# A two-layer decoder trunk on one core: an explicit list of steps, a planned issue order on every engine, and layer 0's values as weights in column tiles

## The chip, the cores and the metric

The kernel runs on one core of a Trainium2 chip. The metric is the device time of one execution in microseconds (us); less is better. Before the change the median of three runs is 644.46 us (641.27 to 646.58).

## The reference, cut to what matters

Two layers work on 256 tokens of width 1024. Layer 0 mixes tokens by blockwise attention with 16 heads of 64 columns; one block holds all 256 tokens here, so it is plain causal attention. Layer 1 mixes by differential attention: 8 heads, each with two score maps and a value of 128 columns. A squared-ReLU MLP of inner width 4096 follows each. Every sub-layer's input is scaled and shifted by vectors made from the conditioning vector `c`, and its output is gated by a third.

```python
mod = jnp.einsum('bd,lde->lbe', jax.nn.silu(c), ada_w) + ada_b[:, None, :]
for i in range(DEPTH):
    shift1, scale1, gate1, shift2, scale2, gate2 = [m[:, None, :] for m in jnp.split(mod[i], 6, axis=-1)]
    h = x * (1.0 + scale1) + shift1
    ...
        y = moba_attention(h, moba_w_in[j], moba_w_out[j])
    ...
        y = diff_attention(h, diff_w_in[j], diff_w_out[j], ...)
    x = layer_norm(DEEPNORM_ALPHA * x + (1.0 + gate1) * y, ln_g[i, 0], ln_b[i, 0])
    h = x * (1.0 + scale2) + shift2
    y = sq_relu_mlp(h, mlp_w_up[i], mlp_w_down[i])
    x = layer_norm(DEEPNORM_ALPHA * x + (1.0 + gate2) * y, ln_g[i, 1], ln_b[i, 1])
```

In layer 0 a head is `p = softmax(q k^T / 8 + causal)`, `o = p v`. In layer 1 it is `w = softmax(q1 k1^T) - lam * softmax(q2 k2^T)`, `o = w v`, then an RMS norm of `o`.

## The kernel before, in words

Tokens stand in two blocks `b` of 128 rows. Every dense product is made of three products of rounded operands: each float32 matrix is split into `hi` (rounded by ScalarE, L131) and `lo` (the rest, by VectorE, L132), and TensorE adds `xh*wh + xh*wl + xl*wh` (L168 to L170 for one PSUM bank, L185 for two). Weights arrive by DMA into three `raw` buffers of 1 MB and are split into eight `hi` and eight `lo` buffers. Scores (L451), transposes through the identity (L400, L431, L510, L321, L116, L705) and the product of probabilities and values (L491) are plain float32 matmuls; the profile shows two records for each of the score and value matmuls.

The work is named by steps, which the string `PROGRAM` lists by layer. V, Q: a 512-column product for values, or for queries and keys of four heads (`g` is the group of four). T: transposes of queries and keys. S: scores and softmax of one block `b` and group `g`. P: transposes of the probabilities, products with the values. F: transposes of the result into operands `sTh`, `sTl` of the output projection. O: output projection. B and C: the gate is spread over the partitions (L116), then LayerNorm and the next modulated input. U, X: MLP up and its transposes. Y: an up step for both blocks at once, with the weights stationary (L724, L729). D: MLP down. E: the last downs of block 1, cut in columns.

The vectors made from `c` cost 96 rows of work: for each of 12 vectors and 8 column blocks, a 0.5 MB DMA into `aw` (two buffers, L216) and a multiply-and-sum on VectorE (L217). Sixteen of them belong to the first layer's input; the other 80 stand in a queue of fillers, `f3` in the list takes three from it, and `need` empties it as far as a step demands.

SP issues all loads and stores, in order. An engine's own queue is in order too: an instruction that waits holds all behind it. Within that, the order in which the instructions of each engine stand is made at build time by the framework's scheduler, which takes the program order as priority; the kernel marks the later scores of a block as urgent and keeps them in program order.

Softmax of layer 0 leaves `p` unnormalised; `sums` (L465, its reciprocal) is applied to the product by VectorE at L502, so the transposes of `p` need only the exponentials. For one head, `p` transposed (128 keys by 128 queries) is the stationary operand and 64 columns of `v` move:

```python
pe.matmul(op[:, h], lhsT=pT[i][kb], rhs=vn[kb, g // 2][:, v0 + h.start:v0 + h.stop], ...)
```

Of the kernel before, what the change touches and what calls it, by code (L numbers as in the profile page):

```python
# [73 lines left out]
def tile_trunk(ctx: ExitStack, tc: tile.TileContext, x, c, moba_w_in, moba_w_out, diff_w_in, diff_w_out,
# [145 lines left out]
    def queue_vector(l, v):  # L220
        cl = small.tile([P, KC], F32, name=f"col{l}{v}")

        def step(j):
            return lambda: ada_rows(l, v, j, cl[:, j:j + 1], "aw", 2)

        def fin():
            if v in (SCALE1, GATE1, SCALE2, GATE2):
                vec.tensor_scalar(out=cl, in0=cl, scalar1=1.0, scalar2=None, op0=ALU.add)
            cols[l, v] = cl

        for j in range(KC):
            filler.append(step(j))
        filler.append(fin)
# [594 lines left out]
```

## Time and profile before

| | us |
|---|---|
| median of 3 runs | 644.46 |
| span of the profiled execution | 639.4 |
| TensorE matmuls busy | 609.9 (95%) |
| VectorE busy | 501.2 (78%) |
| ScalarE busy | 377.4 (59%) |

The page and the times give no device time of the profiled execution beyond its span; the median of the runs is 5.1 us above the span and the fastest run 1.9 us. Matmuls are drawn longer than the distance to the next one (a 512-column matmul about 395 ns, with the next one starting 227 ns later), so the busy share hides gaps of up to some 170 ns: starts are what counts. By time, layer 0's attention ends at about 155 us, its MLP at about 320, layer 1's attention at about 445 and its MLP at about 620; the last 19 us hold the end of the last down projection, LayerNorm and the stores.

### The profile page before, as it was taken

Reading aid. Unit: us, or ns where it says so; the run is one execution under the profiler, and the core shown is the slowest. Engines: PE = TensorE matmul, PEld = TensorE weight load, DVE = VectorE, ACT = ScalarE, POOL = GpSimd, SP = SyncE. Lnnn points to the kernel's source line nnn. Section 1 sums busy time; section 2 is a strip of 40 time slices with the busy share of each in tenths; the row PEclk is TensorE's granted clock in tenths of the full one; section 3 lists DMA queues with packets and bytes.
Section 4 is the critical chain, followed back from the end, with each engine's and each line's share of the span. In section 5 each row is a group of like instructions: output and inputs, shape, how many; then the busy total and the mean of one; then the engine's idle time right before and its main releaser. Section 6 shows DMA issues by size and latency. Waiting matters only on the chain.

```text
span 639.4 us, 8821 instructions
## 1 busy us (share of the span) xinstructions
PE 609.9 (95%) x3164; PEld 501.8 (78%) x3164; DVE 501.2 (78%) x907; ACT 377.4 (59%) x699; POOL 21.2 (3%) x36
## 2 busy tenths in 40 slices
PE   4989999998999999999999999999999999999995
PEld 3767887886888888888877787767788888888884
DVE  5798998979978987887799889877984645565447
ACT  3448666657746564655477676775785556465530
POOL 0000000011000000000000010021100000000001
PEclk9999999999999999999999999999999999999998
DMA  8987988976689988888765967782663764646501
GB/s 294 406 312 288 313 321 292 309 251 224 226 285 361 331 316 312 316 300 335 257 227 189 337 230 242 253 283 66 206 218 109 260 225 152 244 147 202 194 0 67
DMA packets 66086, 158.25 MB, mean 248 GB/s; under 512 B 4057, under 2 KB 21370, under 8 KB 66042
## 3 DMA queue, kind: packets, MB, share of 16 engines
q1 hardware_dynamic: 66042, 157.68, 70.2%
q8 instruction: 25, 0.41, 0.2%
q14 instruction: 19, 0.16, 0.1%
HBM read 156.62 MB, written 1.05 MB: 247 GB/s over the span
## 4 chain that ended last, share of the span: by engine, by line
PE 59%; DVE 21%; DMA 10%; ACT 3%; issue 3%; POOL 2%; SPq 1%; DVEq 0%; ACTq 0%; POOLq 0%
PE ac L185 13%; PE sc L185 10%; DMA aw<-in_ada_w_dram 8%; PE mm L724 7%; PE tp L724 6%; DVE lo L132 6%; DVE aw L217 5%; PE mm L170 4%; PE mm L729 3%; PE mm L168 3%; PE mm L169 3%; PE tp L729 3%; DVE z L293 1%; ACT hi L131 1%; DVE z L290 1%
## 5 line engine op out<-in xcount | busy, mean ns | idle before, releaser
L132 DVE TENSOR_TENSOR lo<-raw,hi 128x1024 fp32r<-128x1024 f32 x196 | 232.1, 1197 | 47.5 <-ACT hi L131 43.6
L131 ACT CAST hi<-raw 128x1024 fp32r<-128x1024 f32 x196 | 201.2, 1034 | 67.0 <-PE sc L185 46.4
L217 DVE CUSTOM_DVE_ANT_0 aw<-aw,sbc,tabT 128x1024 f32<-128x1024 f32 x96 | 121.9, 1279 | 16.4 <-DMA aw<-in_ada_w_dram 16.0
L168 PE MATMUL mm<-hi,hT 128*128 128x512 f32 x224 | 90.6, 405 | 5.3 <-ACT hi L131 2.5
L170 PE MATMUL mm<-hi,hT 128*128 128x512 f32 x224 | 89.1, 398 | 0.0
L169 PE MATMUL mm<-lo,hT 128*128 128x512 f32 x224 | 88.8, 397 | 0.2 <-DVE lo L132 0.2
L724 PE MATMUL mm<-hT,hi 128*128 128x512 f32 x192 | 60.4, 396 | 0.0
L724 PE MATMUL tp<-hT,hi 128*128 128x512 f32 x192 | 60.3, 395 | 0.0
L168 PEld LDWEIGHTS mm<-hi,hT 128*128 128x128 f32 x224 | 42.3, 189 | 15.2 <-ACT hT L555 3.0
L185 PE MATMUL ac<-hi,sTh 128*128 128x512 f32 x160 | 51.2, 397 | 0.0
L185 PE MATMUL ac<-lo,sTh 128*128 128x512 f32 x160 | 50.8, 393 | 0.0
L185 PE MATMUL ac<-hi,sTl 128*128 128x512 f32 x160 | 50.4, 392 | 0.0
L170 PEld LDWEIGHTS mm<-hi,hT 128*128 128x128 f32 x224 | 42.4, 189 | 9.1 <-DVE hT L329 0.4
L169 PEld LDWEIGHTS mm<-lo,hT 128*128 128x128 f32 x224 | 42.4, 189 | 8.6 <-DVE lo L132 0.3
L185 PE MATMUL sc<-hi,sTh 128*128 128x512 f32 x144 | 45.3, 392 | 0.0
L185 PE MATMUL sc<-lo,sTh 128*128 128x512 f32 x144 | 45.2, 391 | 0.0
L185 PE MATMUL sc<-hi,sTl 128*128 128x512 f32 x144 | 44.6, 391 | 0.0
L729 PEld LDWEIGHTS tp<-hT,lo 128*128 128x128 f32 x192 | 34.4, 188 | 7.5
L729 PEld LDWEIGHTS mm<-hT,lo 128*128 128x128 f32 x192 | 34.4, 188 | 7.3
L734 ACT COPY nat<-mm 128x256 f32<-128x256 f32 x24 | 7.8, 376 | 52.4 <-PE mm L724 52.4
L729 PE MATMUL tp<-hT,lo 128*128 128x256 f32 x192 | 36.0, 279 | 0.0
L729 PE MATMUL mm<-hT,lo 128*128 128x256 f32 x192 | 35.9, 279 | 0.0
(169 smaller groups left out, 909.4 us busy)
## 6 DMA issues: line engine op xcount, KB each, us to landing
aw<-in_ada_w_dram SPq DMA_DIRECT2D x96, 512.0 KB, 5.5
raw<-in_mlp_w_up_dram SPq DMA_DIRECT2D x32, 1024.0 KB, 5.5
raw<-in_mlp_w_down_dram SPq DMA_DIRECT2D x32, 1024.0 KB, 4.9
raw<-in_diff_w_in_dram SPq DMA_DIRECT2D x16, 512.0 KB, 4.9
raw<-in_moba_w_in_dram SPq DMA_DIRECT2D x24, 256.0 KB, 5.9
raw<-in_moba_w_in_dram SPq DMA_DIRECT2D x8, 512.0 KB, 4.7
raw<-in_moba_w_out_dram SPq DMA_DIRECT2D x4, 1024.0 KB, 7.8
raw<-in_diff_w_in_dram SPq DMA_DIRECT2D x4, 1024.0 KB, 6.2
```

The lines of the kernel that those rows point to most:

```text
L131: act.copy(out=hi[:, :n], in_=raw_ap)
L132: vec.tensor_tensor(out=lo[:, :n], in0=raw_ap, in1=hi[:, :n], op=ALU.subtract)
L168: pe.matmul(dst, lhsT=xh, rhs=wh, start=start, stop=False)
L169: pe.matmul(dst, lhsT=xh, rhs=wl, start=False, stop=False)
L170: pe.matmul(dst, lhsT=xl, rhs=wh, start=False, stop=stop)
L185: pe.matmul(dsts[h], lhsT=a, rhs=w[:, h * 512:(h + 1) * 512], start=start and k == 0 and i == 0, stop=stop and k == n - 1 and i == 2)
L217: vec.tensor_tensor_reduce(out=aw, in0=aw, in1=sbc, scale=1.0, scalar=adab_cols(l, v)[:, j:j + 1], op0=ALU.mult, op1=ALU.add, accum_out=dst)
L290: vec.tensor_tensor(out=z[:, c_], in0=accs[c_.start // 512][:, a0:a0 + c_.stop - c_.start], in1=gate[:, c_], op=ALU.mult)
L293: vec.scalar_tensor_tensor(out=z[:, c_], in0=xt[b][:, c_], scalar=ALPHA, in1=z[:, c_], op0=ALU.mult, op1=ALU.add)
L724: pe.matmul(ps, lhsT=w[k][0][:, c_], rhs=x3[k], start=first, stop=last)
L729: pe.matmul(ps[:, 0:S], lhsT=w[k][1][:, c_], rhs=x3[k][:, 0:S], start=False, stop=False)
L734: act.copy(out=r[:, i * S:(i + 1) * S], in_=ps[:, S:2 * S])
```

## The change

Three things change.

First, the list. One list of explicit steps replaces the two: a step names its layer, the filler queue is gone and each of its 80 rows is a step of its own (`a024`: layer 0, vector 2, column block 4), weight loads are steps of their own (`q02`, `o00`, `u03`, `d05`), and B is cut into G (gate), K (rows of the LayerNorm's weights) and N (scale and shift columns); R is the residual. Steps of the next stage stand inside the one before.

Second, the order. The instructions are recorded in the order of the list, and then `plan_issue` walks them with a table of durations and latencies: of the instructions whose inputs and buffers its own clock says are ready, each engine takes the first in the list. `issue_in_order` then ties each instruction to the one before it on its engine, on all five of them. The urgent marks on the scores go. On TensorE the planner keeps half-array matmuls next to each other.

Third, layer 0's values. `attend_values_T` multiplies `p` by the reciprocal sums on ScalarE ahead of the transposes, and then makes the transposed result directly: 64 columns of `v` are the stationary operand, the 128 queries move, and two heads write the two halves of the partitions (column tiles of 64). So layer 0 has no F step and no multiplication by `sums` on VectorE; `split_oT` reads the product where it read the transposes.

```diff
-    L0 V00 V10 Q00 T00 Q10 T10 Q01 T01 Q11 T11 S0 V01 f2 S1 f1 P0 S2 V11 f5 P1 F0 S3 P2 Q02 T02 f4 S4
...
+    Q001 V000 a031 a037 a030 T001 Q000 Q011 S02 a024 a042 a022 q02 a021 T011 S03 a025 Q010 T010 T000 V010 S01
...
+    def forward(self, prio, wait_ns=0.0):
...
+            c = cand[e]
+            pick = None
+            if e == 4 and pair[lastpe] and lastpe + 1 < N and pair[lastpe + 1]:
+                for x in c:
+                    if x[1] == lastpe + 1 and x[2] <= t + 60:
+                        pick = x
+            if pick is None:
+                lim = t + wait_ns
+                pick = min([x for x in c if x[2] <= lim])
...
+def plan_issue(ins, slots, psum_names):
+    p = Planner(ins, slots, psum_names)
+    p.forward(list(range(p.N)))
+    return p.orders
...
+def pairable(i):
+    return not i.is_transpose and tuple(i.tile_size) in ((64, 128), (128, 64))
+
+
+def issue_in_order(tc, ins, orders):
+    for o in orders:
+        for a, b in zip(o, o[1:]):
+            tc.add_manual_dep(ins[b], ins[a].name,
+                              mybir.DependencyInfo(mybir.DependencyClass.NoSync, mybir.DependencyReason.DATA),
+                              reason="planned order")
...
+    def step_ada(st, l, v, j):
+        if (l, v) not in cols:
+            cols[l, v] = small.tile([P, KC], F32, name=f"col{l}{v}")
+        cl = cols[l, v]
+        ada_rows(l, v, j, cl[:, j:j + 1], "aw", 2)
...
-                    first = i == kb == 0 and cpt == 1
-                    with nullcontext() if first else tc.high_priority():
-                        mm = pe.matmul(r[i, cpt][:, kb * P:(kb + 1) * P], lhsT=qk[b, g][rows, i, :],
-                                       rhs=qk[kb, g][rows, 2 + i, :], start=True, stop=True)
-                        if not first:
-                            tc.keep_in_program_order(mm)
+                    pe.matmul(r[i, cpt][:, kb * P:(kb + 1) * P], lhsT=qk[l, b, g][rows, i, :],
+                              rhs=qk[l, kb, g][rows, 2 + i, :], start=True, stop=True)
...
+    def attend_values_T(b, g, ps_, sums):
+        n = P * (b + 1)
+        v0 = (g % 2) * 256
+        oT_ps = psum("ac" if g < 2 else "mm")
+        for i in range(2):
+            pair = ps_[2 * i:2 * i + 2]
+            for cpt, pt in enumerate(pair):
+                c_ = 2 * i + cpt
+                act.activation(out=pt[:, :n], in_=pt[:, :n], func=AF.Copy, scale=sums[:, c_:c_ + 1])
+            pT = probs_T(b, pair)
+            for kb in range(b + 1):
+                for cpt in range(2):
+                    h0 = v0 + (2 * i + cpt) * HD
+                    pe.matmul(oT_ps[cpt * HD:(cpt + 1) * HD, i * P:(i + 1) * P], lhsT=vn[0, kb, g // 2][:, h0:h0 + HD],
+                              rhs=pT[cpt][kb], start=kb == 0, stop=kb == b)
+        split_oT(0, b, g, oT_ps)
...
+    ins = [i for i in nc.cur_bb.bb.instructions if i.opcode != "TilePoolBoundary"]
+    issue_in_order(tc, ins, plan_issue(ins, slots, psum_names))
```

The order moves at three places that the prediction speaks of. On TensorE, at the end of layer 0's attention, the rows before are these (L431 transposes `p`, L491 multiplies by the values, L510 transposes the result, L185 is the output projection into `ac` for block 0 and `sc` for block 1).

```order
L185 MATMUL ac<-lo,sTh 128x512 x2
L185 MATMUL ac<-hi,sTl 128x512 x2
L431 MATMUL tp<-cs,p 128x128 x8
L185 MATMUL sc<-hi,sTh 128x512
L491 MATMUL mm<-v,pT 128x64 x8
L510 MATMUL tp<-cs,on 128x128 x2
L185 MATMUL sc<-hi,sTh 128x512
L185 MATMUL sc<-lo,sTh 128x512
L510 MATMUL tp<-cs,on 128x128 x2
L185 MATMUL ac<-hi,sTh 128x512 x2
```

The rows at the same place now (L765 transposes `p`, L852 multiplies by the values, L538 is the output projection):

```order
L538 MATMUL sc<-hi,sTh 128x512 x2
L765 MATMUL tp<-cs,p 128x128 x2
L538 MATMUL sc<-lo,sTh 128x512
L765 MATMUL tp<-cs,p 128x128 x2
L538 MATMUL sc<-lo,sTh 128x512
L765 MATMUL tp<-cs,p 128x128 x2
L538 MATMUL sc<-hi,sTl 128x512
L765 MATMUL tp<-cs,p 128x128 x2
L538 MATMUL sc<-hi,sTl 128x512
L852 MATMUL mm<-pT,v 64x128 x4
L538 MATMUL sc<-hi,sTh 128x512 x2
```

The transposes of the result are gone, the transposes of `p` stand between matmuls of the output projection, and block 0's projection (`ac`) is over before the last transposes of `p`, where twelve of its matmuls stood behind them before.

On VectorE, at the end of layer 1's attention, the rows before (L217 are rows of the conditioning vectors, L476 and L473 finish a softmax, L502 normalises a result, L520 splits it):

```order
L502 TENSOR_TENSOR on<-mm,ss 128x256
L476 SCALAR_TENSOR_TENSOR p<-p,sums_4144 128x256
L217 ISA aw,col_526<-aw,sbc,tabT 128x1024
L217 ISA col_526 128x1
L473 RECIPROCAL sums_4157<-sums_4157 128x2
L474 TENSOR_TENSOR sums_4157<-sums_4157,nlam 128x1
L520 SCALAR_TENSOR_TENSOR sTl<-tp,sgcol,sTh 128x2x128
L217 ISA aw,col_526<-aw,sbc,tabT 128x1024
L217 ISA col_526 128x1
L476 SCALAR_TENSOR_TENSOR p<-p,sums_4157 128x256
```

and now (L803, L804 and L806 finish a softmax, L834 normalises, L873 splits):

```order
L834 TENSOR_TENSOR on<-mm,ss 128x256
L804 TENSOR_TENSOR sums_4220<-sums_4220,nlam 128x1
L803 RECIPROCAL sums_4233<-sums_4233 128x2
L804 TENSOR_TENSOR sums_4233<-sums_4233,nlam 128x1
L806 SCALAR_TENSOR_TENSOR p<-p,sums_4220 128x256
L806 SCALAR_TENSOR_TENSOR p<-p,sums_4233 128x256
L873 SCALAR_TENSOR_TENSOR sTl<-tp,sgcol,sTh 128x2x128
```

The rows of the conditioning vectors have left this place. Of the 96 rows in the whole order, 40 stand up to the end of layer 0's first LayerNorm before and now; 36 follow up to layer 0's second LayerNorm before, and 42 now; 20 stand from there to layer 1's first LayerNorm before, and 14 now.

On SP, in layer 0's MLP, the rows before:

```order
L146 DMA raw<-in_mlp_w_up_dram 128x4x512
L216 DMA aw<-in_ada_w_dram 128x1024 x2
L146 DMA raw<-in_mlp_w_up_dram 128x4x512
L216 DMA aw<-in_ada_w_dram 128x1024
L160 DMA raw<-in_mlp_w_down_dram 128x2x1024
```

and now:

```order
L562 DMA aw<-in_ada_w_dram 128x1024 x2
L513 DMA raw<-in_mlp_w_down_dram 128x2x1024
L562 DMA aw<-in_ada_w_dram 128x1024 x4
L513 DMA raw<-in_mlp_w_down_dram 128x2x1024
L562 DMA aw<-in_ada_w_dram 128x1024
```

Up to four loads into `aw`, which has two buffers, now stand ahead of a weight load.

More of the change, by code (lines that the diff above doesn't have):

```diff
@@ L62, in _schedule @@
+"""
 def _schedule():
-    for part in PROGRAM:
-        for t in part.split():
-            yield (t[0],) + tuple(int(d) for d in t[1:])
+    for t in PROGRAM.split():
+        yield (t[0],) + tuple(int(d) for d in t[1:])
 SHIFT1, SCALE1, GATE1, SHIFT2, SCALE2, GATE2 = range(6)
@@ L70, with __init__, tile, _access @@
 C_W = 576
+class SlotPool:
+    def __init__(self, pool, slots):
+        self.pool, self.slots = pool, slots
+    def tile(self, shape, dtype, tag=None, name=None, bufs=1):
+        t = self.pool.tile(shape, dtype, tag=tag or name, name=name, bufs=bufs)
+        self.slots[(t.tensor if hasattr(t, "tensor") else t).name] = (tag or name, bufs)
+        return t
+def _access(a):
+    a = getattr(a, "bass_ap", None)
+    if a is None:
+        return None
+    t = a.tensor
+    if type(t).__name__ != "Tile":
+        return None
+    size = 1
+    for n in t.shape[1:]:
+        size *= n
+    p0, f0 = divmod(a.offset, size)
+    np_ = a.ap[0][1]
+    pm = 0
+    for q in range(p0 // 32, (p0 + np_ + 31) // 32):
+        pm |= 1 << q
+    g = max(1, size // 64)
+    free = [(s, n) for s, n in a.ap[1:] if n > 1 and s]
+    run = free.pop()[1] if free and free[-1][0] == 1 else 1
+    offs = [f0]
+    for s, n in free:
+        offs = [o + s * i for o in offs for i in range(n)]
+    fm = 0
+    for o in offs:
+        lo, hi = o // g, (o + run - 1) // g
+        fm |= ((1 << (hi - lo + 1)) - 1) << lo
+    return t.name, pm, fm
@@ new lines, in _transfer, with run @@
+def _transfer(i):
+    o, s_ = i.outs[0], i.ins[0]
+    def run(dims):
+        r = 1
+        for s, n in reversed(dims):
+            if n > 1:
+                if s != r:
+                    break
+                r *= n
+        return r
+    store = type(s_.bass_ap.tensor).__name__ == "Tile"
+    on, off = (s_, o) if store else (o, s_)
+    r = run(list(on.ap)[1:])
+    if not any(s == 0 and n > 1 for s, n in off.ap):
+        r = min(r, run(list(off.ap)))
+    return o.ap[0][1] * _elems(o) / r / 16 * (8 + r * 4 * 0.0368) * 1.03
@@ L125, in tile_trunk @@
         xt.append(xb)
+    xs = {(b, 0): xt[b] for b in range(2)}
     def split_piece(raw_ap, n=1024):
@@ L218, in ada_rows @@
                                  op0=ALU.mult, op1=ALU.add, accum_out=dst)
[L220 to L233, printed above, removed]
-    def need(key):
-        while key not in cols:
-            fill()
+    def step_ada(st, l, v, j):
[3 more added lines that the diff above has]
+        ada_rows(l, v, j, cl[:, j:j + 1], "aw", 2)
+        if j == KC - 1 and v in (SCALE1, GATE1, SCALE2, GATE2):
+            vec.tensor_scalar(out=cl, in0=cl, scalar1=1.0, scalar2=None, op0=ALU.add)
     def affine_cols(l, first, prev):
         sc, sh = (l, SCALE1 if first else SCALE2), (l, SHIFT1 if first else SHIFT2)
-        need(sc)
-        need(sh)
         A = small.tile([P, KC], F32, name=f"A{l}{int(first)}")
@@ L638, in close @@
             return
[L639 to L641 removed]
+        z = layer_norm(b, accs, gate, xs[b, 2 * l + i])
+        modulate(b, z, *st["ab", l, i], tiles)
+        st["z", l, i, b] = z
     def run(program, st):
```

476 lines of the change are left out of this document (352 added, 124 removed).

## The prediction

> **What bounds the kernel now.** I read the busy times by stretch first, then TensorE's groups, then TensorE's timeline where stages meet, then the rows of VectorE. Columns of the stretches: length, then busy time of PE, PEld, DVE, ACT and POOL with counts, granted clock, DMA share, GB/s.
>
> ```profile
> 0.00:40.00 40.00, 29.18 (x115) 22.23 (x115) 28.51 (x55) 17.20 (x33) 0.29 (x5) 1.00 0.96 357
> 40.00:160.00 120.00, 115.50 (x660) 92.52 (x660) 108.63 (x253) 77.99 (x176) 3.30 (x4) 1.00 0.81 283
> 160.00:320.00 160.00, 160.00 (x808) 135.68 (x807) 133.20 (x181) 91.76 (x130) 0.00 (x0) 1.00 0.85 304
> 320.00:460.00 140.00, 133.65 (x707) 105.59 (x706) 124.58 (x288) 95.96 (x225) 15.02 (x24) 1.00 0.65 225
> 460.00:620.00 160.00, 160.00 (x808) 135.40 (x808) 91.34 (x103) 93.48 (x138) 0.00 (x0) 1.00 0.53 180
> 620.00:639.40 19.40, 11.56 (x76) 10.39 (x73) 14.90 (x30) 1.02 (x2) 2.55 (x3) 0.90 0.15 55
> ```
>
> Both MLPs (160 to 320, 460 to 620) keep TensorE busy without a gap. The first 40 us run at a DMA share of 0.96. What is left to win lies in the two attentions, 40 to 160 and 320 to 460: TensorE shows 4.50 + 6.35 us idle there, and VectorE 11.4 + 15.4 us, so VectorE is nearly as full as TensorE.
>
> Idle by the page is not all, since a matmul's row is drawn beyond the start of the next. So I count slots from start to start. The chain of waits gives the wide one, the timeline at 606 us a period of two wide and two half-wide matmuls, and the one at 70 us the small ones.
>
> ```profile
> 260.99 5.45 PE ac L185 x24
> 266.44 5.44 PE sc L185 x24
> ```
>
> ```profile
> 606.32 0.40 PE L729 MATMUL tp<-hT,lo 128*128 128x256 f32 x2
> 606.55 0.63 PE L724 MATMUL tp<-hT,hi 128*128 128x512 f32 x2
> ...
> 607.02 0.39 PE L729 MATMUL tp<-hT,lo 128*128 128x256 f32 x2
> ```
>
> ```profile
> 69.26 0.40 PE L170 MATMUL mm<-hi,hT 128*128 128x512 f32 x1
> 69.59 0.49 PE L451 MATMUL sc<-qkT 64*128 64x128 f32 x2
> 70.00 0.51 PE L168 MATMUL mm<-hi,hT 128*128 128x512 f32 x1
> ...
> 74.37 0.40 PE L170 MATMUL mm<-hi,hT 128*128 128x512 f32 x1
> 74.70 1.16 PE L451 MATMUL sc<-qkT 64*128 64x128 f32 x16
> 75.79 2.00 PE L491 MATMUL ac<-v,pT 128*128 128x64 f32 x16
> 77.62 0.39 PE L510 MATMUL tp<-cs,on 128*128 128x128 f32 x2
> ```
>
> A wide slot is 5.45/24 = 0.227 us; the period is 0.70. Sixteen value records (L491) take 1.83, 0.114 each. A burst of score matmuls in half arrays costs 0.10 to enter (74.70 - 74.37 - 0.227) and 1.09 for 16 records, 1.19 for 8 matmuls; a burst of one costs 0.10 + 0.41 = 0.51. Between these, a burst of m matmuls is about 0.41 + 0.0975 m.
>
> ```profile
> L168 PE MATMUL mm<-hi,hT 128*128 128x512 f32 x194 | 77.6, 401 | 1.9 <-ACT hT L328 1.1 <-ACT hT L555 0.8
> ...
> L185 PE MATMUL ac<-hi,sTh 128*128 128x512 f32 x96 | 31.4, 401 | 0.0
> ...
> L724 PE MATMUL mm<-hT,hi 128*128 128x512 f32 x96 | 30.2, 396 | 0.0
> ...
> L729 PE MATMUL tp<-hT,lo 128*128 128x256 f32 x96 | 18.0, 279 | 0.0
> ...
> L451 PE MATMUL sc<-qkT 64*128 64x128 f32 x192 | 16.9, 291 | 0.0
> ...
> L321 PE MATMUL tp<-cs,z 128*128 128x128 f32 x44 | 6.9, 280 | 3.2 <-DVE nm L311 1.8 <-DVE z L309 1.5
> L510 PE MATMUL tp<-cs,on 128*128 128x128 f32 x32 | 6.4, 281 | 1.4 <-ACT gate L118 0.7 <-DVE sums L473 0.5 <-DVE on L502 0.2
> ```
>
> These are groups between 40 and 460 us. There are 618 wide matmuls on L168 to L170 (three lines of 194 and twelve of each third in `sc` and `ac`), 576 on L185 (six groups of 96), 192 and 192 in L724 and L729, and 396 narrow ones. Slots: 1194 x 0.227 = 271.0; 96 periods of 0.70 = 67.2; 396 x 0.11 = 43.6; the scores, in 20 bursts of the old order (four of 1, three of 3, five of 4, one of 7, seven of 8), 17.6. Sum 399 of 420 us: about 20 us of waits, of which the MLP between them has hardly 1. The releasers named beside L321 and L510 are VectorE and ScalarE; nothing waits for a weight load by DMA.
>
> **Part 1, layer 0's values on TensorE.** Before: 48 matmuls, two records each, 96 x 0.114 = 10.9 us. Now they come in twelve bursts (two of 2, nine of 4, one of 8). No row shows column tiles; the nearest are the row tiles of the scores. By those: 2 x 0.61 + 9 x 0.80 + 1.19 = 9.6. Sixteen transposes go, 16 x 0.11 = 1.8. The scores come in 23 bursts now (twelve of 2, four of 4, seven of 8): 18.8, so +1.2. Together -1.3 - 1.8 + 1.2 = **-2 us**. The upper end is no overlap between tiles: 10.9 again plus twelve switches of 0.3, +3. The lower end is a free switch: the 16 records of 1.09 us give 0.068 each, 6.5 in all, and then -5.
>
> The Trainium skill ("TensorEngine Tiling (Array Packing)", Theoretical Speedup) allows up to twice the rate where one side is 64; halving 10.9 would make the part -6, and no run here shows it yet.
>
> **Part 2, VectorE in the attentions.**
>
> ```profile
> 40.00:160.00 120.00, 35.78 (x56) 1.00 0.81 283
> 160.00:320.00 160.00, 46.11 (x72) 1.00 0.85 304
> 320.00:460.00 140.00, 25.58 (x40) 1.00 0.65 225
> ```
>
> ```profile
> L502 DVE TENSOR_TENSOR on<-mm,sums 128x256 f32<-128x256 f32 x4 | 1.7, 423 | 2.7 <-PE mm L491 2.7
> L502 DVE TENSOR_TENSOR on<-ac,sums 128x256 f32<-128x256 f32 x4 | 1.7, 418 | 0.0
> ```
>
> The first three rows are L217 alone, two records a row of work: 25.58/20 = 1.28 us. Six such rows leave layer 1's attention, 7.7 us. L502 leaves layer 0's, 3.4 us. With as much idle time on VectorE as now, 26.8 us, the two stretches would shrink by these 11.1. TensorE allows it: it has some 19 us of waits there. The order adds a little at the LayerNorm of layer 0, where L321 and its like wait: between the end of block 0's projection and the transposes of its LayerNorm stood 45 wide slots, 10.2 us; now 42, eight transposes of `p`, two bursts and four transposes of the gate, 9.5 + 0.9 + 1.6 + 0.4 = 12.4. I take 2 of the 3.2 us. Together **-13 us**, -2 of which are the chance of the new order and the rest of the load. Ends: -1 (waits only change places) and -19 (all of them go).
>
> **Part 3, what is added, and what hides it.** ScalarE multiplies 32 maps in layer 0.
>
> ```profile
> L475 ACT ACTIVATE p<-p,sums 128x256 f32<-128x256 f32 x8 | 4.1, 507 | 1.5 <-DVE sums L474 1.4
> ...
> L475 ACT ACTIVATE p<-p,sums 128x128 f32<-128x128 f32 x8 | 3.2, 402 | 1.0 <-DVE sums L474 1.0
> ```
>
> 16 x 0.507 + 16 x 0.402 = 14.5 us on an engine with 78 of 120 busy: hidden if TensorE has other work. It lies in the chain, though: the transposes of a pair needed two exponentials, and now need four, their reciprocal and two products (price below). Six more L217 rows in layer 0's MLP make 7.7 us on VectorE, 133.2 to 141 of 160, and 3.1 MB more for the DMA, share 0.85 to about 0.90, below the 0.96 of the first stretch: hidden, 0; if that cover goes, up to 8. The runs of four `aw` loads ahead of a weight load hold SP until VectorE has freed two buffers, about 4 x 1.28 = 5 us, while the weights ahead of it feed a period of two sets of 48 wide slots, 22 us. The first 40 us load the same bytes in nearly the same order: 0, ends -1 and +1. The tail has the same VectorE steps behind the last matmul: 0.
>
> **Sum.** -2 - 13 = -15 against the span of 639.4: 624. The median of the runs is 5 us above the span; scaled, 644.5 x 624.4/639.4 = 629. The unknown costs span -5 - 19 - 1 = -25 to +3 - 1 + 8 + 1 = +11.
>
> **Rivals.**
>
> Same: VectorE sets both attentions and the new order only moves the waits, as any in-order queue with 1.2 us steps may. For it: VectorE is 90% busy in both. Against: six rows and L502 do leave. It gives part 1 and 2 to 3 us, 640.
>
> Slower: the longer softmax chain is not covered in layer 0.
>
> ```profile
> L418 ACT ACTIVATE p<-sc,mx 128x256 f32<-128x256 f32 x32 | 15.0, 476 | 7.8 <-DVE mx L415 7.0 <-DVE sums L474 0.6
> L415 DVE CUSTOM_DVE_ANT_0 sc<-sc,cs 128x256 f32<-128x256 f32 x32 | 13.2, 436 | 1.0 <-ACT p L418 0.9
> ...
> L418 ACT ACTIVATION_READ_ACCUMULATOR p<-sc,mx 128x1 f32 x64 | 12.9, 202 | 0.0
> ...
> L415 DVE DVE_READ_ACCUMULATOR2_ANT mx<- 128x1 f32 x64 | 9.0, 141 | 0.0
> ...
> L465 DVE RECIPROCAL sums<-sums 128x4 f32<-128x4 f32 x8 | 1.4, 173 | 0.6 <-ACT p L418 0.5
> ```
>
> For block 1 the two extra maps cost 2 x (0.436 + 0.141) on VectorE and one exponential with its sum, 0.68, then 0.17 and 2 x 0.507: 3.0 us more before the transposes; I take 2.7 over both blocks. Eight times is 22, and with layer 1's 8 us still won and part 1 kept the end is 644 + 22 - 10 = 656. It decides where fewer than about 4 x 0.58 + 0.68 + 0.17 + 1.0 = 4.2 us of other matmuls stand between scores and transposes. At the last block 15 wide slots, sixteen transposes and two value bursts stand there, 3.4 + 1.8 + 1.6 = 6.8 us: against it.
>
> Column tiles that don't overlap.
>
> ```profile
> L491 PEld LDWEIGHTS mm<-v,pT 128*128 128x128 f32 x72 | 9.0, 191 | 1.4 <-ACT pT L433 1.1
> ```
>
> If the load of one tile's weights can't run beside the other tile's matmul, a pair of records takes 0.19 + 0.11 = 0.30; 48 pairs and twelve switches of 0.3 make 18.0, 7.1 more than before, and part 1 becomes +6.5: 644.5 - 6.5 = 638. The Trainium skill ("TensorE: Matmul & The Clock Gate", What overlaps and what doesn't) says that weight loads overlap running matmuls only where the row groups differ, and two column tiles share all their rows. The rows here, with tiles that differ in rows, can't tell.
>
> **How the numbers follow.** About 1% is what a measurement of this kernel can tell from no change: 638 to 651. Forecast, 620 to 637: 0.62. Column tiles that don't overlap, 638: 0.08, half of it faster. Same, 640: 0.20. Slower, 656: 0.08. All waits gone and tiles at full rate, below 620: 0.02. So faster 0.68, within 1% 0.24, slower 0.08. The range reaches from just under the forecast's end to the cases of no change: 618 to 643.
>
> **What would show it.** Right: TensorE's busy time falls to about 601 (624 less 19 at both ends and 4 in the attentions), VectorE's by 3.4 in all; the stretch that was 320 to 460 shortens by 8 or more, that of layer 0's attention by 4 or more; layer 0's MLP stays at 160 us with TensorE full; the value matmuls come 0.07 us apart in a burst. Wrong: TensorE waits on ScalarE's scaled `p` or on weights in layer 0's MLP; VectorE idles more than 27 us in the attentions; or value matmuls stand 0.11 us apart or more.

## The result and the profile after

The changed kernel takes 650.19 us (median of 4 runs, 649.63 to 650.67) against 642.87 for the kernel before on the same chip: a ratio of 1.0115 (95% interval 1.0077 to 1.0153). It is slower by about 1%; 629 was forecast, with a range of 618 to 643. The profiled execution has a span of 647.8 us, 8.4 more than before.

The busy times by stretch of the changed kernel, with columns as before:

```profile
40.00:160.00 120.00, 116.14 (x639) 88.40 (x638) 103.19 (x241) 87.13 (x205) 5.02 (x4) 0.99 0.80 280
160.00:320.00 160.00, 152.95 (x758) 125.68 (x757) 136.22 (x186) 90.94 (x130) 0.00 (x0) 1.00 0.87 313
320.00:460.00 140.00, 138.00 (x728) 111.41 (x727) 116.22 (x276) 94.20 (x223) 17.34 (x22) 1.00 0.61 210
460.00:620.00 160.00, 159.84 (x806) 134.19 (x806) 92.53 (x107) 93.18 (x139) 2.49 (x2) 1.00 0.54 185
```

Layer 0's MLP, where TensorE had 808 matmul records in 160 us, now has 758. At the mean distance of 160/808 = 0.198 us the 50 missing ones are 9.9 us. Layer 1's MLP is untouched (806 against 808). To see whole stages, I take the time from the first transposes of block 1's LayerNorm to those of block 0's next one. For layer 0's MLP these are two rows of TensorE's timeline before,

```profile
154.59 0.33 PE L321 MATMUL tp<-cs,z 128*128 128x128 f32 x1 [0.47 <-DVE z L309]
...
325.56 0.41 PE L321 MATMUL tp<-cs,z 128*128 128x128 f32 x2 [0.95 <-DVE nm L311]
```

and two after:

```profile
156.55 0.33 PE L654 MATMUL tp<-cs,z 128*128 128x128 f32 x1
...
338.05 0.41 PE L654 MATMUL tp<-cs,z 128*128 128x128 f32 x2 [1.72 <-DVE nm L644]
```

So the stage was 171.0 us and is 181.5. Read off in the same way:

| stage, us | before | after |
|---|---|---|
| start to the end of layer 0's attention | 154.6 | 156.6 |
| layer 0's MLP | 171.0 | 181.5 |
| LayerNorm | 13.0 | 12.7 |
| layer 1's attention | 107.8 | 104.0 |
| LayerNorm | 13.0 | 12.7 |
| layer 1's MLP | 171.9 | 172.2 |
| from the last matmul to the end | 8.1 | 8.1 |

Three stages are longer by 10.5, 2.0 and 0.3 us, the others shorter by 3.8 and 0.6: 8.4 in all. The loss is nearly all in one stage, layer 0's MLP; the gain of layer 1's attention is half the forecast one, and layer 0's attention gained nothing. The conditioning rows moved as the order said (L563 alone, two records a row; before 56, 72 and 40):

```profile
40.00:160.00 120.00, 35.68 (x56) 0.99 0.80 280
160.00:320.00 160.00, 48.85 (x79) 1.00 0.87 313
320.00:460.00 140.00, 21.70 (x34) 1.00 0.61 210
```

What waits in layer 0's MLP between 160 and 320 us (engine, line, what ended the wait: total us, times, longest) was this before,

```profile
DVE aw L217 <- DMA aw<-in_ada_w_dram: 11.1, 7, 4.3
```

and is this after:

```profile
DVE aw L563 <- DMA aw<-in_ada_w_dram: 16.0, 13, 2.5
...
ACT hi L484 <- DMA raw<-in_mlp_w_down_dram: 6.7, 3, 3.3
PEld ac L538 <- DVE lo L485: 5.9, 5, 2.0
...
PE ac L538 <- DVE lo L485: 3.8, 4, 1.5
```

VectorE stands longer and more often at a row whose data has not landed; the weight splits (`lo`, L485) are queued behind that row on VectorE, and now TensorE waits for them, which it hardly did before. One such place, first on VectorE and then on TensorE (the first number is the start, the one in brackets the wait):

```profile
222.77 1.28 DVE L563 CUSTOM_DVE_ANT_0 aw<-aw,sbc,tabT 128x1024 f32<-128x1024 f32 x1 [1.80 <-DMA aw<-in_ada_w_dram]
...
223.98 1.22 DVE L485 TENSOR_TENSOR lo<-raw,hi 128x1024 fp32r<-128x1024 f32 x1
```

```profile
225.25 0.73 PE L538 MATMUL ac<-lo,sTh 128*128 128x512 f32 x2 [1.55 <-DVE lo L485]
```

The other change is in the scores. The timeline of TensorE in the changed kernel at three bursts, each with what follows it:

```profile
75.96 0.66 PE L852 MATMUL ac<-pT,v 128*64 128x128 f32 x8
76.55 0.50 PE L522 MATMUL mm<-lo,hT 128*128 128x512 f32 x1
...
77.92 1.71 PE L783 MATMUL sc<-qkT 64*128 64x128 f32 x16
79.56 0.50 PE L521 MATMUL mm<-hi,hT 128*128 128x512 f32 x1
...
82.12 0.71 PE L783 MATMUL sc<-qkT 64*128 64x128 f32 x4 [1.59 <-ACT p L752]
82.75 0.50 PE L521 MATMUL mm<-hi,hT 128*128 128x512 f32 x1
```

Eight records of the column tiles (L852) take 76.55 - 75.96 = 0.59 us, and the two records of a pair start 6 to 7 ns apart: the two tiles overlap. But these sixteen records of the scores take 1.64, where the prediction's row gave 1.09, and four take 0.63. The old order let the two halves of the array take turns. In the new one the marks that kept the scores in program order are gone, and the planner takes whichever half has a free bank, so several matmuls of one half follow each other and don't overlap (the first five records of this burst start 111 ns or more apart). Counted from start to start with their entries, the scores take 24.2 us instead of 18.1, the column-tile values 9.1.

### The profile page after: what moved, and what is told of

The parts are those of the page before. It is cut to its first block, busy times and chain, and to the rows that moved or that the text cites. A ratio compares the mean times of both kernels' runs of the same rounds, so it can differ in the third digit from the quotient of the medians.

```text
span 647.8 us, 8858 instructions
## 1 busy us (share of the span) xinstructions
PE 615.0 (95%) x3148; PEld 498.2 (77%) x3148; DVE 498.6 (77%) x899; ACT 387.4 (60%) x731; POOL 27.7 (4%) x36
## 4 chain that ended last, share of the span: by engine, by line
PE 58%; DMA 16%; DVE 15%; issue 4%; ACT 4%; POOL 2%; SPq 0%; DVEq 0%; ACTq 0%; POOLq 0%
PE ac L538 11%; DMA aw<-in_ada_w_dram 11%; PE sc L538 9%; PE mm L522 5%; PE mm L521 5%; PE mm L523 5%; DVE lo L485 5%; DVE aw L563 4%; PE mm L1069 4%; PE tp L1069 4%; DMA raw<-in_moba_w_in_dram 3%; PE sc L783 3%; ACT hi L484 2%; PE tp L1074 2%; PE mm L1074 2%
## 5 line engine op out<-in xcount | busy, mean ns | idle before, releaser
L485 DVE TENSOR_TENSOR lo<-raw,hi 128x1024 fp32r<-128x1024 f32 x196 | 231.0, 1198 | 61.4 <-ACT hi L484 59.9
L563 DVE CUSTOM_DVE_ANT_0 aw<-aw,sbc,tabT 128x1024 f32<-128x1024 f32 x96 | 121.9, 1281 | 27.0 <-DMA aw<-in_ada_w_dram 26.9
L522 PE MATMUL mm<-lo,hT 128*128 128x512 f32 x224 | 90.5, 405 | 0.7 <-DVE lo L485 0.7
L538 PE MATMUL ac<-lo,sTh 128*128 128x512 f32 x160 | 50.9, 398 | 3.8 <-DVE lo L485 3.8
L538 PE MATMUL ac<-hi,sTh 128*128 128x512 f32 x160 | 50.7, 397 | 1.5 <-ACT hi L484 1.5
L538 PE MATMUL ac<-hi,sTl 128*128 128x512 f32 x160 | 51.2, 397 | 0.0
L522 PEld LDWEIGHTS mm<-lo,hT 128*128 128x128 f32 x224 | 42.7, 190 | 10.4 <-DVE lo L485 2.1
L538 PE MATMUL sc<-hi,sTl 128*128 128x512 f32 x144 | 45.8, 394 | 1.4 <-DVE sTl L1086 1.4
L538 PE MATMUL sc<-hi,sTh 128*128 128x512 f32 x144 | 46.2, 395 | 0.0
L538 PE MATMUL sc<-lo,sTh 128*128 128x512 f32 x144 | 45.8, 392 | 0.0
L538 PEld LDWEIGHTS ac<-lo,sTh 128*128 128x128 f32 x160 | 29.3, 188 | 11.7 <-DVE lo L485 5.9
```

What stands on the lines that cost most here:

```text
L485: vec.tensor_tensor(out=lo[:, :n], in0=raw_ap, in1=hi[:, :n], op=ALU.subtract)
L522: pe.matmul(dst, lhsT=xh, rhs=wl, start=False, stop=False)
L538: pe.matmul(dsts[h], lhsT=a, rhs=w[:, h * 512:(h + 1) * 512], start=start and k == 0 and i == 0, stop=stop and k == n - 1 and i == 2)
L563: vec.tensor_tensor_reduce(out=aw, in0=aw, in1=sbc, scale=1.0, scalar=adab_cols(l, v)[:, j:j + 1], op0=ALU.mult, op1=ALU.add, accum_out=dst)
```

## The experiments

Two theories for the MLP came first: **rows** (42 instead of 36 conditioning rows are too many for that stage) and **landing** (the time from a load's issue until its data can be used: the fixed order places rows on VectorE by a landing of 4.0 us, `1530 + 1310 + 1150` ns, which the loads don't keep). The rest of the loss was to be **pairing** of the scores or the **chain** (ScalarE's products ahead of the transposes). All kernels compute the whole reference. Ratios are to the kernel before on the same chip; "MLP 0", "att 1" and so on are the stages of the table, from one profiled execution each.

### One part alone on the old kernel

**e_columns**: only `attend_values_T`.

```diff
+        if kind == 0:
+            return attend_values_T(b, g, ps_, sums)
```

> The kernel before, with layer 0's values in column tiles alone (scaled p, no F step in layer 0), order by the framework's scheduler. If the column tiles overlap as the changed kernel's trace shows (a burst of four matmuls 0.68 to 0.80 us with its entry, 96 records in 8.7 us against 10.7) and sixteen transposes go (1.8), TensorE loses about 4 us: 639 against 643, less if VectorE sets layer 0's attention (641). If the longer softmax chain (exponentials, reciprocal, two products) is what cost the change its time, 646 or more.

Measured: 642.92, ratio 1.0008 (0.9985 to 1.0031). The first two stretches:

```profile
40.00:160.00 120.00, 111.38 (x639) 85.65 (x639) 105.86 (x244) 87.17 (x205) 3.30 (x4) 0.99 0.80 281
160.00:320.00 160.00, 160.00 (x807) 135.63 (x807) 133.28 (x181) 92.49 (x132) 0.00 (x0) 1.00 0.85 303
```

TensorE is busy 4.1 us less in layer 0's attention (115.50 before) and VectorE 2.8 us less, and the stage is no shorter (156.3 at its end, 154.6 before). The work that leaves both engines doesn't come back as time. Of TensorE's waits between 40 and 160 us the two longest are these; the longest before was 1.1 us:

```profile
PE ac L185 <- DVE lo L132: 2.9, 1, 2.9
PE mm L522 <- ACT pT L433: 2.2, 1, 2.2
```

The first is for a weight split, and the granted clock behind it is 0.51 from 107 to 110.5 us (1.00 before), 1.7 us more. The second is the column tiles (L522) waiting for ScalarE's copies of the transposed `p`. So ScalarE has its extra 9 us, and a chain that costs 22 is refuted; 2.2 us of it can be seen, and with the split they use up the gain of this execution.

**e_halves**: the old kernel with its scores half by half.

```diff
-        for i in range(2):
-            for kb in range(b + 1):
-                for cpt in (1, 0):
-                    rows = slice(cpt * 64, (cpt + 1) * 64)
+        for cpt in (1, 0):
+            rows = slice(cpt * 64, (cpt + 1) * 64)
+            for i in range(2):
+                for kb in range(b + 1):
```

> The kernel before, with the score matmuls recorded half by half: all of rows 64 to 127 first, then all of rows 0 to 63, instead of in turn. Theory 'halves': matmuls in the same half do not overlap, a burst of 16 records takes 1.73 us with its entry instead of 1.18 and one of 8 records 1.19 instead of 0.75; 8 x 0.55 + 8 x 0.44 = 8 us more on TensorE, the time 5 to 8 us longer (648 to 651). Rival: TensorE waits in the attentions anyway, the time at most 2 us longer.

Measured: 643.66, ratio 1.0029 (1.0009 to 1.0049); scores 21.8 us instead of 18.1. Unpaired scores cost the old order 2 us, less than expected: the 3.7 us partly fill waits.

### Pairing, rows and landing in the changed kernel

**e_pair**: the planner keeps the scores in list order and starts a group only when both banks are free.

```diff
+        rows = [k for k in range(N) if self.pair[k] and ins[k].tile_size[0] == 64]
+        self.heads = set(rows) - {k + 1 for k in rows}
+        for j, k in zip(rows, rows[1:]):
+            preds[k].setdefault(j, False)
...
+                if first[q[qpos[tag]]] in self.heads:
+                    if len(freeat[tag]) < 2:
+                        return
```

> The changed kernel, whose planner keeps the score matmuls in program order (the two halves in turn) and starts a group only when both of its banks are free. Theory 'halves': score bursts fall from 23 us to about 15.4 (eight of 0.74, eight of 1.19), the attentions together get 5 to 8 us shorter, 642 to 645 against 650; layer 0's MLP keeps its 181 us. Rival: the wait for two banks delays the softmax as much, 649 to 652.

Measured: 643.51, ratio 1.0028 (1.0001 to 1.0054). In its timeline sixteen records again take 1.1 us:

```profile
69.95 1.16 PE L793 MATMUL sc<-qkT 64*128 64x128 f32 x16
```

The scores take 16.5 us in all, layer 0's attention ends at 152.8 instead of 156.6, and by the two ratios the time falls by 0.9% against the change. Layer 0's MLP stays long, 180.2. So pairing is one of two causes, worth some 5 to 7 us.

**e_rows**: the six added rows moved in the list behind layer 0's second LayerNorm and held there.

```diff
...
-    N01 a156 C001 q10 D016 D017 C011 q11 Q100 ...
+    N01 C001 q10 D016 D017 C011 a151 a145 a135 a142 a133 a156 q11 Q100 ...
...
```

> The changed kernel, with six rows of the conditioning vectors moved from layer 0's MLP behind its end and held there (36 rows in the MLP and 20 in layer 1's attention, as in the kernel before). Theory 'rows': the ring of two buffers (load 6 to 8 us, then 1.28 us on VectorE) carries no more than about 40 rows in that stage; with 36 the MLP falls from 181.5 to 172 to 175 us, and layer 1's attention gets 0 to 6 longer: 642 to 649. Theory 'landing': the plan counts on a load landing 4.0 us after its issue where 6 to 8 are seen, so rows stand too early on VectorE whatever their number: the MLP stays at 178 or more, 648 to 653.

Measured: 665.31, ratio 1.0362 (1.0324 to 1.0400). MLP 0 is 176.0, half of the loss gone; but the six rows stand together ahead of layer 1's first weights, that attention takes 119.1, and TensorE waits for splits there:

```profile
PEld mm L529 <- DVE lo L492: 6.5, 4, 2.8
```

It shows what rows ahead of weight splits cost, and settles nothing on the MLP.

**e_dma**: the planner counts 6.2 us for the landing of a row's load, and 12% more time per byte. The edit holds for all loads, weights too.

```diff
-                dma = max(s + 1530, dma) + self.bytes_[k]
-                end[k] = dma + 1150
+                dma = max(s + 1530, dma) + 1.12 * self.bytes_[k]
+                end[k] = dma + 3200
```

> The changed kernel, whose planner counts on slower loads: 357 GB/s instead of 400 and 2.05 us more from the transfer's end to its use, so a 512 KB load lands 6.2 us after its issue instead of 4.0. Theory 'landing': rows and splits on VectorE no longer stand ahead of loads that are still under way; the wait of L217's successor for DMA in layer 0's MLP falls from 22 us to below 10 and the MLP from 181.5 to 172 to 176, the time to 641 to 645. Theory 'rows' (40 rows still stand in the MLP): it stays at 179 or more, 648 to 651.

Measured: 671.62, ratio 1.0436 (1.0390 to 1.0481). VectorE's waits on `aw` in the MLP fall to 2.4 us and TensorE waits for no split there, as landing says, with two buffers and 39 rows. But the stage takes 187.8 us: the same list with a slower planned ring delivers the vectors of the LayerNorms too late. Between 140 and 170 us one finds:

```profile
PE tp L654 <- ACT full L658: 10.4, 1, 10.4
ACT full L658 <- DVE nm L644: 10.0, 1, 10.0
```

**e_pairdma**, both edits at once, gives 664.83 (1.0329, 1.0291 to 1.0367): the gain of pairing stays, the loss too.

> Both mends together: score matmuls in pairs, a group starting only with both banks free, and the planner's loads landing after 6.2 us. If the two losses are separate they add: 643.5 less another 5 to 8, 636 to 639, which would beat the kernel before (641.5). If layer 0's MLP is short of DMA rate rather than of room for late loads, 641 to 644.

**e_noplan**: the changed kernel without the planned order (the framework's scheduler orders the new list).

```diff
-    issue_in_order(tc, ins, plan_issue(ins, slots, psum_names))
```

> The changed kernel without its plan: the new list and the column tiles, the issue order left to the framework's scheduler as in the kernel before. If the plan makes the loss, layer 0's MLP falls to 171 to 175 us and the score bursts to about 20: 638 to 644. If the list makes it (the rows of the conditioning vectors stand where they did, 40 in that MLP), 647 to 653.

Measured: 662.85, ratio 1.0282 (1.0234 to 1.0331), MLP 0 177.5. By the two ratios the plan is worth 1.7%, 11 us, to this list; it is the list that brings the extra rows.

**e_aw3**: three `aw` buffers in the changed kernel, one of five q/k buffers given up for them.

```diff
-        ada_rows(l, v, j, cl[:, j:j + 1], "aw", 2)
+        ada_rows(l, v, j, cl[:, j:j + 1], "aw", 3)
-        t = ap_.tile([P, 4, P], F32, tag="qkT", name="qkT", bufs=5)
+        t = ap_.tile([P, 4, P], F32, tag="qkT", name="qkT", bufs=4)
```

> The changed kernel with three buffers for the rows of the conditioning vectors instead of two (room from one buffer of transposed queries and keys less, a smaller pad, and a tail tile that shares a tag). The plan now puts 51 rows into layer 0's MLP. Theory 'ring of two': two buffers carried 42 rows in 181 us, 4.3 us a row; with three a row takes 2.9 and 51 rows fit in 170: the MLP is 172 to 177 us. Theory 'DMA rate': 4.7 MB more at a share of 0.87 make the MLP 185 or longer.

Measured once: 658.75. The planner now draws 50 rows into MLP 0, which takes 179.7 all the same, with a DMA share of 0.91. So the DMA's rate was not the limit at 42 rows.

### The same rows in the old order

**e_sixrows**: the old kernel, old scheduler, and only more fillers in layer 0's MLP, so that VectorE has 42 rows there and 14 in layer 1's attention, as in the changed kernel.

```diff
-    O11 C10 ... f1 X11 Y2 f4 D10 f1 D01 f1 D11 Y3 f3 D02 f1 D12 Y4 f3 D03 f1
+    O11 C10 ... f1 X11 Y2 f4 D10 f2 D01 f2 D11 Y3 f6 D02 f2 D12 Y4 f6 D03 f2
...
```

> The old kernel with its old order and scheduler, but with six more conditioning rows drawn into layer 0's MLP (42 on VectorE there instead of 36, 14 instead of 20 in layer 1's attention), spread over the stage. If the count of rows through two aw buffers is what costs in that MLP, the stage grows from 171 to 178 to 181 us, layer 1's attention loses 4 to 7, and the time is 643 to 649. If only the fixed order that trusts too short a landing costs, the stage stays at 171 to 174 us, layer 1's attention loses as much, and the time is 636 to 641.

Measured: 650.87, ratio 1.0150 (1.0114 to 1.0185). MLP 0 grows from 171.0 to 179.9, and layer 1's attention becomes 1.3 us shorter. Six rows alone do the harm that the forecast priced at nothing. SP's waits between 160 and 320 us show how; before,

```profile
SPq L216 <- DVE col L217: 51.0, 29, 5.2
SPq L146 <- DVE lo L132: 45.6, 13, 8.3
SPq L160 <- DVE lo L132: 28.2, 13, 3.8
```

and in e_sixrows:

```profile
SPq L216 <- DVE col L217: 89.9, 33, 5.0
...
SPq L146 <- DVE lo L132: 18.3, 4, 8.3
SPq L160 <- DVE lo L132: 5.8, 3, 2.5
```

L216 issues a row's load and waits until VectorE has read the buffer; L146 and L160 issue weight loads and wait until a `raw` buffer is free, which is lead. The lead goes from 73.8 us of waiting to 24.1, and then ScalarE waits for weights (over the whole stage; before, the view has only 2.1 us, for the up projection's):

```profile
ACT hi L131 <- DMA raw<-in_mlp_w_down_dram: 28.8, 9, 5.3
```

**e_sixaw3**: the same with a third `aw` buffer (edit of e_aw3).

> The old order with the extra rows in layer 0's MLP (41 there) and a third buffer for the conditioning loads (one buffer of q and k fewer, which may cost layer 0's attention 2 to 4). Ring theory: with two buffers SP stands 90 us behind rows that VectorE has not read yet and the weight loads stand behind it; a third buffer brings the stage back from 179.9 to 171 to 174, time 640 to 645. Bandwidth theory: with two buffers this stage moved 304 to 309 GB/s in every order, and it stays at 178 to 181, time 647 to 651.

Measured: 650.48, ratio 1.0134 (1.0100 to 1.0169). The stage is back at 169.2 us with 41 rows and 315 GB/s between 160 and 320 us (302 in e_sixrows). Over the whole stage the rates are 320 and 300 GB/s, so both move 54 MB in it, and the work has not just left the stage: in the old order it is the ring of two buffers that carries the loss there, not the DMA. The weight loads have their lead again:

```profile
SPq L216 <- DVE col L217: 63.4, 28, 5.2
SPq L146 <- DVE lo L132: 32.1, 11, 5.8
SPq L160 <- DVE lo L132: 28.5, 10, 6.1
```

The time doesn't fall, because layer 0's attention now ends at 164.7 instead of 156.4; the last section shows why.

**e_late**: the old kernel, with the eight rows of the last vector held until a weight load of layer 1's MLP, and one filler fewer in layer 1's list (rows by stage 40, 36, 12, 8).

```diff
+        if (l, v) == (1, GATE2):
+            tc.add_manual_dep(nc.cur_bb.bb.instructions[-1], gate[0].name, ...)
```

> The old kernel with the eight rows of its last conditioning vector taken out of layer 1's attention into layer 1's MLP, where VectorE and the DMA are half idle (VectorE's rows by stage: 40, 36, 12, 8). VectorE theory: 8 x 1.28 = 10.2 us leave a stage that VectorE bounds, layer 1's attention shortens by 4 to 10 of its 107.8 us, layer 1's MLP stays at 172, time 633 to 639. Rival, by what the column tiles alone did: less work on one engine only moves waits there, at most 1 us, time 641 to 643.

Measured: 641.30, ratio 0.9985 (0.9960 to 1.0009). The rows did leave (25.58 us of L217 in that stretch before):

```profile
320.00:460.00 140.00, 16.84 (x28) 1.00 0.59 204
```

Layer 1's attention is 104.9 instead of 107.8: 2.9 us for 10.2 us of VectorE work.

**e_late3** (e_late with the third buffer of e_aw3) and **e_latebc** (e_late with the third buffer taken from the LayerNorm's three row buffers instead, the row of `ln_b` moving into the `aw` ring) were to be faster than both kernels.

```diff
-        t = ap_.tile([P, D], F32, tag="bc", name="bc", bufs=3)
+        t = ap_.tile([P, D], F32, tag=tag, name=tag, bufs=bufs)
...
-        bb = load_bcast(ln_b[l, i:i + 1, :])
+        bb = load_bcast(ln_b[l, i:i + 1, :], "aw", 3)
```

> The old order and scheduler, the last vector's eight rows in layer 1's MLP, and three buffers for the conditioning loads (VectorE's rows by stage 42, 41, 5, 8). Ring theory: layer 0's MLP 171 to 174, layer 1's attention 101 to 104 by the 0.3 us a row that the run with the late rows gave, time 636 to 641. Bandwidth theory: layer 0's MLP 178 to 180, time 644 to 648.

> The old order and scheduler with the same third buffer and the last vector's rows in layer 1's MLP. Ring theory: layer 0's MLP 169 to 171, layer 0's attention as before at 115 to 118 (its loss in e_late3 came from the buffers of q and k), layer 1's attention 105, time 637 to 642. If the third buffer itself costs the attention by more rows there, 645 or more.

Measured: 648.07 (1.0087, 1.0056 to 1.0119) and 648.71 (1.0103, 1.0072 to 1.0134). MLP 0 is 169.2 and 170.2, as the ring theory has it, but layer 0's attention ends at 165.3 and 164.2. My reason for that (the lost q/k buffer) was wrong, since e_latebc keeps it. Layer 1's attention is 104.8 with 5 rows on VectorE (e_late3) and 104.9 with 12 (e_late): in the old order, fewer rows than 12 bring nothing more there.

### The ring and the landing together in the changed kernel

**e_pair15**: e_pair, with the last vector's rows held until layer 1's MLP (rows by stage 40, 37, 11, 8).

```diff
-    a123 a153 S12 T111 ... a155 q12 S13 ...
+    a123 S12 T111 ... q12 S13 ...
...
+    ... C110 a150 a151 a152 a153 a154 a155 a156 a157 U100 ...
```

> The changed kernel with paired scores and the eight rows of the last vector held until layer 1's MLP (VectorE's rows by stage about 40, 38, 11, 7 instead of 40, 43, 13, 0). Rows theory: layer 0's MLP comes from 180 to 175 to 177, layer 1's attention stays near 103, time 636 to 640. Rival, landing alone: that MLP stays at 180, time 642 to 645.

Measured: 643.62, ratio 1.0023 (0.9993 to 1.0054). MLP 0 falls only to 177.9 with 37 rows; the old order has 36 in 171.0. Layer 1's attention gains 2, its MLP loses 3 (175.2).

**e_pairbc** (the edits of e_pair and the third buffer of e_latebc) and **e_pair15bc** (e_pair15 and that buffer):

> The changed kernel with paired scores and a third buffer for the conditioning loads, taken from the LayerNorm's three (one of its broadcast rows moves into the conditioning ring, so the buffers of q and k stay); 42 rows in layer 0's MLP as in e_pair. Ring theory: that stage falls from 180.2 to 170 to 174 and the time from 643.5 to 633 to 638, faster than both kernels. If the planned order's short landing is what costs there, the stage stays above 177 and the time at 640 to 645.

> As e_pairbc, with the last vector's eight rows held until layer 1's MLP (rows 36, 11, 8 in the three later stages). Ring theory: layer 0's MLP 170 to 173, layer 1's attention 101 to 103, layer 1's MLP 172 to 175, time 632 to 637. Short landing: layer 0's MLP 176 or more, time 638 to 643.

Measured: 642.74 (1.0002, 0.9974 to 1.0030) and 646.60 (1.0064, 1.0043 to 1.0086). MLP 0 stays at 181.6 and 179.5, and the wait on the rows stays too. Between 160 and 320 us in e_pairbc:

```profile
DVE aw L573 <- DMA aw<-in_ada_w_dram: 18.3, 12, 2.6
```

So the third buffer, which helped in the old order, is not enough in the planned one, and fewer rows are not either (36 rows in e_pair15bc). What is left is where the plan puts them.

**e_bcmid** and **e_bcdma**: e_pairbc with another landing in the planner, 5.0 us for a row's load in the first, the 6.2 us of e_dma in the second, and as much more for the weight loads.

```diff
-                end[k] = dma + 1150
+                end[k] = dma + 2200
```

> e_pairbc (paired scores, three buffers), and the planner counts 5.0 us from issue to landing for a conditioning load instead of 4.0 (1.53 + 1.31 + 2.2); that alone moves rows on the planned orders (38 in layer 0's MLP, 17 in layer 1's attention). Landing theory: rows stand later on VectorE, its waits on their loads in that stage fall from 23 to under 12, the stage from 181.6 to 172 to 176, layer 1's attention gains 2, time 634 to 641. If the landing counts for nothing once there is a third buffer, the stage stays above 179, time 642 to 646.

> e_pairbc with the landing of e_dma (6.2 us, and 357 GB/s). With two buffers this made layer 0's MLP dense but brought the vectors of the LayerNorms late by 35 us in all and cost 28 us. Landing theory: with three buffers the vectors come in time, the stage is 170 to 175, layer 0's attention 155 to 160 at its end, time 634 to 644. Rival: the rows of the list's order come too late whatever the ring, 655 to 670.

Measured: e_bcmid 639.63, ratio 0.9960 (0.9939 to 0.9981). One number takes MLP 0 from 181.6 to 169.4 us, and its stretch is as full as in the old kernel:

```profile
160.00:320.00 160.00, 160.00 (x804) 134.47 (x803) 134.78 (x186) 91.83 (x128) 0.10 (x1) 1.00 0.86 309
```

VectorE's waits on rows there fall from 18.3 us to 3.2:

```profile
DVE aw L573 <- DMA aw<-in_ada_w_dram: 3.2, 4, 1.2
```

Layer 1's attention pays 5 of the 12 us back (107.1; it has 17 rows instead of 13). The plan moved rows too (38 instead of 42 in layer 0's MLP), but e_pair15bc has 36 with the short landing and keeps its loss. The time falls by less than the stages: 3.1 us by the medians, where the profiled execution of e_pairbc is the slowest of its ten and that of e_bcmid the fastest. e_bcdma gives 655.91 (1.0194, 1.0156 to 1.0232): 6.2 us is too much for this list even with three buffers. Its vectors come late at layer 0's second LayerNorm: TensorE stands idle for 16 us between 320 and 360 us, 14.7 of them in front of the transposes of the gate and of the LayerNorm, and not at all from 154 to 320.

By the ratios e_bcmid is faster than the change by 1.5%, and than the kernel before by 0.4%, the only version that beats both. Whether two buffers do with a landing of 5.0 us was not tried, nor a later landing for the rows or the weights alone.

## Why the prediction was wrong

**Layer 0's MLP, part 3** ("below the 0.96 of the first stretch: hidden, 0; if that cover goes, up to 8"). This step failed first. The busy share of the DMA was the wrong cover: loads of rows go through two buffers and in turn with weight loads on one queue, and six more rows take two thirds of the lead that the weight loads had (73.8 us to 24.1 in e_sixrows). They cost 8.9 us in the old order, through the ring (e_sixaw3). In the changed kernel the stage's 10.5 us come through the fixed order, planned by a landing of 4.0 us: VectorE stands at rows that have not landed, and with a later landing the stage is dense again (e_pairbc against e_bcmid, 181.6 to 169.4 us). How much of that is the rows' landing and how much the weights' is not shown. The landing stood in the code, and the profile's DMA list showed another:

```profile
aw<-in_ada_w_dram SPq DMA_DIRECT2D x96, 512.0 KB, 5.7
```

Those are the median us of the changed kernel; before they were 5.5. The prediction looked for SP holding weights back (5 us against a lead of 22) and not for rows that hold the splits behind them on VectorE.

**The score bursts, part 1** (23 bursts, "so +1.2"). The bursts were counted right and priced by rows in which the halves alternate; in the new order they mostly don't. They cost +6.1 instead of +1.2, and pairing them again brings back 0.9% (e_pair).

**The values, part 1** (10.9 to 9.6, transposes -1.8). Right in size: 9.1 us, tiles overlap, and that rival is out. The Trainium skill ("TensorE: Matmul & The Clock Gate", What overlaps and what doesn't) lets weight loads overlap running matmuls only where row groups differ; the records of L852 here use all 128 rows in both tiles and overlap all the same. The Trainium skill ("TensorEngine Tiling (Array Packing)", Key Properties) says that different tiles can load and multiply in parallel, and with that the trace agrees (0.59 us for eight records that took 0.91 before). On the clock the part was worth nothing by itself (e_columns: +0.1%, -0.15 to +0.31).

**VectorE in the attentions, part 2** ("With as much idle time on VectorE as now ... shrink by these 11.1"). The direction is right in layer 1's attention and the size was not: six rows fewer and the whole new order gave 3.8 us of the 7.7, six rows alone 1.3 (e_sixrows), e_late 2.9 of 10.2, and e_late3 nothing for seven rows more. In layer 0's attention the 3.4 us of L502 left and nothing came of it. So VectorE, busy for 90% of these stages, gave back between a sixth and a half of what was taken from it, and soon nothing. Of the 2 us at the LayerNorm, TensorE's waits in front of its transposes (L321, now L654) show 1.2: they fell from 3.3 to 2.1 us in all.

**What held**: ScalarE's products are nearly hidden, the tail is the same (8.1), and so is layer 1's MLP (0.3 longer).

**Rivals and range.** "Same: ... the new order only moves the waits" described both attentions best. The slower rival had the sign and not the mechanism: in the changed kernel one wait of 1.59 us on ScalarE's `p` at 82 us and 0.5 us on `pT` are all its chain shows. The ends of the sum, -25 to +11, reached to 655 and held the result; the range of 618 to 643 cut off the +8 of part 3, and that is the term that came, at 10.5. The signs named for a wrong forecast ("TensorE waits ... on weights in layer 0's MLP") are what the trace showed, by way of the splits on VectorE; TensorE's busy time is 615.0 instead of 601.

## What to carry to other kernels

Before work is moved into a stage that looks open by busy shares, count what its loads must pass: buffers in the ring, turns on the queue, and what stands behind the waiting instruction on its engine. A fixed order is as good as the latencies it was planned with: compare them with the profile's time to landing, and try values between, since too long a one starves the next stage. When marks that kept an order are dropped, look in the new order for what they held together.

## What the runs showed of the chip

**Halves and tiles.** Score matmuls that alternate between the halves of the array take 1.09 us for sixteen records, those of one half mostly in a row 1.64.

**A short wait can cost more than itself.** In the changed kernel TensorE stands from 80.36 (one slot after its last matmul) to 82.12 us, and a little later the clock falls; the granted clock is the third number from the end:

```profile
80.00:83.00 3.00, 1.41 (x8) 0.79 (x6) 3.00 (x13) 2.98 (x12) 0.00 (x0) 1.00 0.52 180
83.00:86.00 3.00, 3.00 (x10) 2.21 (x10) 3.00 (x11) 0.68 (x2) 0.00 (x0) 0.59 0.23 48
86.00:89.00 3.00, 3.00 (x14) 2.40 (x13) 0.48 (x4) 2.33 (x5) 0.00 (x0) 0.84 0.89 281
```

Six us at a mean of 0.72 are 1.7 us more on top of the 1.76. It does not always come: waits of 1.49, 1.55 and 1.72 us in the same kernel (up to 195.36, 225.25 and 338.05 us) were followed by a clock of 1.00, where the profile gives 1.59 for the one at 82.12. What decides is not shown. In e_latebc the clock falls between 100 and 120 us, where its attention loses time, behind a gap of 2.60 us:

```profile
109.09 0.69 PE L404 MATMUL tp<-cs,nat 128*128 128x128 f32 x4 [2.60 <-DVE nat L397]
```

The clock by stretch there:

```profile
106.00:109.00 3.00, 0.49 (x3) 0.07 (x1) 2.87 (x10) 1.68 (x3) 0.00 (x0) 1.00 0.91 277
109.00:112.00 3.00, 2.91 (x14) 2.49 (x15) 3.00 (x3) 2.06 (x4) 0.00 (x0) 0.59 0.89 314
112.00:115.00 3.00, 3.00 (x16) 2.41 (x15) 0.66 (x3) 0.74 (x2) 0.00 (x0) 0.50 0.82 273
```

The Trainium skill ("TensorE: Matmul & The Clock Gate", HAM oscillation — how this bites in real kernels) warns of gaps over about 3.4 us; here one of 1.76 us, and in e_latebc one of 2.60, were followed by the lower clock.

VectorE's timeline in e_latebc shows what TensorE waits for at 109.09: three rows stand on VectorE ahead of the last step of `nat`.

```profile
104.30 1.28 DVE L221 CUSTOM_DVE_ANT_0 aw<-aw,sbc,tabT 128x1024 f32<-128x1024 f32 x1
...
105.50 1.28 DVE L221 CUSTOM_DVE_ANT_0 aw<-aw,sbc,tabT 128x1024 f32<-128x1024 f32 x1
...
107.46 1.28 DVE L221 CUSTOM_DVE_ANT_0 aw<-aw,sbc,tabT 128x1024 f32<-128x1024 f32 x1
...
108.66 0.28 DVE L397 TENSOR_TENSOR nat<-nat,rtmp 128x128 f32<-128x128 f32 x1
```

e_sixaw3 has the same three rows, and `nat` at 109.17; e_late3 has them too. Between 40 us and the end of layer 0's attention, TensorE's waits for `nat` and for `lo` are 3.4 and 2.4 us in e_latebc, 0.4 and 0.2 before. That the third buffer lets the scheduler put these rows together fits the three kernels that have it in the old order, and was not tested apart from it.
